# Ranking a hybrid decoder's side TensorE work 30 instructions behind its place

## The chip, the cores and the metric

The kernel runs on one core of one Trainium2 chip. A core has a matrix engine (TensorE; PE in the profile, PEld for its weight loads), a vector engine (VectorE, DVE), a scalar engine (ScalarE, ACT), GpSimd (POOL), and SyncE (SP), whose queue issues nearly all DMA transfers here. TensorE writes into PSUM banks. The metric is device time of one launch in microseconds: 2443.29 us, the median of three runs (2434.94, 2443.29 and 2444.47).

## The reference

One layer of a hybrid decoder trunk: a prompt of 2048 tokens and eight sample tokens (one new token each, with caches), width 1024, in float32. Cut to what matters:

```
h    = rms_norm(x, norm1_w)
q, k, v, z, xbc, dt_raw = split(h @ w_in)
a    = sliding-window attention(q, k, v)        # window 128, sinks, relative bias
xbc  = silu(causal_conv(xbc)); xs, B, C = split(xbc)
s    = chunked state-space scan(xs, dt, B, C)   # chunks of 128, state carried on
s    = group_rms_norm((s + xs * D) * silu(z))
x    = x + concat(a, s) @ w_out
h2   = rms_norm(x, norm2_w)
x    = x + (silu(h2 @ w_gate) * (h2 @ w_up)) @ w_down
y    = rms_norm(x, final_norm_w)
```

Beside y, the last window of keys and values, the last convolution rows and the scan's state are returned.

## The kernel before

Tokens are cut into six groups: 2, 3, 3, 3, 3 and 2 blocks of 128 (256 or 384 columns), the last with the eight sample tokens (264 columns). Every activation lies with features on partitions and tokens along the free axis. For accuracy each float32 factor of a projection is split into a rounded high part and a remainder, and three products are summed: high by high, high by low, low by high. So one 128-feature output tile of a 1024-deep projection is 24 matmuls into one PSUM bank (`proj`, L232, `mm3`). A weight tile comes in two halves of 512 KB from a copy that an earlier group has stored already split (tile `w`, tag `w2`, five buffers, L203), or, when first met, as raw 256 KB halves (`wraw`, L206) that ScalarE rounds (L207) and GpSimd or VectorE subtracts (L210); the split pair is stored for later groups (L214).

The work of a group is written as stages, Python generators that emit some instructions and yield:

- I and X load the tokens and form the normed, split pair (I for group 0, X for the others);
- A projects x, B, C and dt and runs the convolution; K projects keys and values; B projects q and z;
- P is attention, Q the scan and its group norm, Y the sample tokens: together the mixers;
- S splits the mixers' output; O is the output projection with the residual; H the second norm; F the FFN, 44 gate and up units with the down projections between them; Z the final norm and the store of y.

A norm's sum over partitions is a matmul with a matrix of ones (`rinv_b`, L683), whose ScalarE and VectorE steps (L693 to L701) then give the factor.

`run` (L1067) steps one main stage a unit at a time, and after each unit lets side stages advance by a given number of steps. `tick` (L188) first emits work that `later` (L185) has set down as due: evictions, the dt rows and sums, transposes of v. In the steady state F of group i is the main stage, with the mixers of group i+1 (spread over `RM` = 53 units) and X of group i+2 beside it; then K and A of group i+2 with S of group i+1 and Z of group i; then O of group i+1; then B of group i+2 with H of group i+1 (L1116 to L1131). Before group 0's F, the groups are filled in by hand (L1101 to L1115). In the last but one F, the S, O and H of the last group are side stages too (L1130).

The order in which each engine executes is not the order of emission. The kernel is built in a tile context with `schedule_with_timeline_sim=True`: every emitted instruction gets the next rank (the context's `cur_priority`), and a planner, which plays the program on a model of the machine, gives each engine the ready instruction of lowest rank. That order is then fixed; on the chip each engine works through its own list and waits at semaphores. Main projections use the PSUM tag `d` (four banks, `psd` in the profile), mixers and norms the tag `m` (four banks, `psm`). The mixers' small buffers share tag `m2` (eight), and x1 and the convolution's tile share tag `x1` (two).

```
    V, S, G, PE, SP = nc.vector, nc.scalar, nc.gpsimd, nc.tensor, nc.sync
    def mm(o, l, r, start=True, stop=True):
        PE.matmul(o, l, r, start=start, stop=stop)
```

All matmuls go through `mm` and so have one line, L104; transposes are `PE.transpose` at L426, L473, L608, L728, L735 and in Y.

Of the kernel before, what the change touches and what calls it, by code (L numbers as in the profile page):

```python
# [27 lines left out]
UQ = 5  # L28
RH0 = 3
DM = 1024  # L30
KT = DM // P
NH = 8
EPS = 1e-6
# [30 lines left out]
def ff_chunks(nf):  # L64

    r = [list(range(f, min(f + FC, nf))) for f in range(0, nf, FC)]
    if len(r) > 1 and len(r[-1]) == 1:
        r[-2:] = [r[-2] + r[-1]]
    return r


@with_exitstack
def hymba(ctx: ExitStack, tc: tile.TileContext, I: dict, O: dict, groups):
    nc = tc.nc
# [4 lines left out]
    chunks = ff_chunks(NF)  # L79
    c_off = [c[0] * DM for c in chunks]  # L80

# [6 lines left out]
    def T(shape, dtype=F32, tag=None, bufs=1):  # L88
        cnt[0] += 1
        nm = f"{tag}_{cnt[0]}"  # L90
        return sb.tile(shape, dtype, tag=tag, name=nm, bufs=bufs)

    def PS(tag):
        cnt[0] += 1
        return pp.tile([P, 512], F32, tag=tag, name=f"ps{tag}_{cnt[0]}", bufs=4)
# [2 lines left out]
        cnt[0] += 1  # L98
        return dr.tile(shape, F32, tag=tag, name=f"{tag}_{cnt[0]}", bufs=bufs)

    V, S, G, PE, SP = nc.vector, nc.scalar, nc.gpsimd, nc.tensor, nc.sync

    def mm(o, l, r, start=True, stop=True):
        PE.matmul(o, l, r, start=start, stop=stop)  # L104
# [65 lines left out]

    wdr = T([P, KT, NH], tag="wdr")
    wdt = T([P, KT, 2 * NH], F32R, tag="wdt")

# [14 lines left out]
    def tick():  # L188
        clock[0] += 1
        now = sorted((d for d in due if d[0] <= clock[0]), key=lambda d: d[:2])  # L190
        due[:] = [d for d in due if d[0] > clock[0]]
        for d in now:
            d[2]()
# [31 lines left out]
    def mm3(o, w, x, k, N, start, stop):  # L225
        whi, wlo = w
        xhi, xlo = x
        mm(o, whi, xhi[:, k, :N], start, False)
        mm(o, whi, xlo[:, k, :N], False, False)
        mm(o, wlo, xhi[:, k, :N], False, stop)  # L230

    def proj(w, x, N, bank="d"):  # L232
        ps = PS(bank)
        for k in range(KT):
            mm3(ps[:, :N], w[k], x, k, N, k == 0, k == KT - 1)
        return ps

    def act_pair(home):
        return tuple(T([P, KT, NMAX], F32R, tag=home + part) for part in ("hi", "lo"))

# [26 lines left out]
    def stage_x(g):  # L267
        N, off = g["N"], g["off"]
        x = g["x"] = act_pair("a")
        xr = T([P, KT, NMAX], tag="xr")  # L270
        for h in range(2):
# [4 lines left out]
        yield from squares(xr, sq, N)  # L276
        yield from rinv_b(sq, N, DM)
        yield from scaled(xr, S_N1, sq, N, x, lambda m: xr[:, m, :N])


    def stage_x0(g):
# [18 lines left out]
        for m in range(KT):  # L300
# [3 lines left out]
            if m % 4 == 3:  # L304
                yield
        yield from rinv_b(r, N, DM)

# [15 lines left out]
    def squares(x, sq, N):  # L323
        t = None
        for m in range(KT + 1):
            if t is not None:
                total(sq, t, N)
            t = T([P, NMAX], tag="tmp", bufs=6) if 0 < m < KT else None
            if m < KT:
                square(x, m, sq if m == 0 else t, N)  # L330
            yield

    def scaled(x, c, r, N, pair, to):

        ts = {}

        def low(m):
            e = G if m % 2 else V
            e.tensor_tensor(pair[1][:, m, :N], ts[m], pair[0][:, m, :N].bitcast(F32), ALU.subtract)  # L339

        for m in range(KT + 2):
            if m >= 2:
                low(m - 2)
            if 1 <= m <= KT:
                S.activation(pair[0][:, m - 1, :N], ts[m - 1], AF.Copy)
            if m < KT:
                ts[m] = to(m)
                V.scalar_tensor_tensor(ts[m], x[:, m, :N], col(c, m), r[:, :N], ALU.mult, ALU.mult)  # L348
            yield
# [333 lines left out]
    def rinv_b(ss, N, d):  # L683

        ss = [s[:, :N] for s in (ss if isinstance(ss, list) else [ss])]
        ps = []
        for s in ss:
            ps.append(PS("m"))
            mm(ps[-1][:, :N], ones, s)
        yield  # L690
        v = [T([P, NMAX], tag="tmp", bufs=6)[:, :N] for _ in ss]
        for s, p in zip(ss, ps):
            S.activation(s, p[:, :N], AF.Ln, bias=epsc[:, 0:1], scale=1.0 / d)  # L693
        for s, u, p in zip(ss, v, ps):
            S.activation(u, p[:, :N], AF.Copy, bias=-0.5 * EPS, scale=-0.5 / d)
            S.activation(s, s, AF.Exp, scale=-0.5)  # L696
        yield
        for s, u in zip(ss, v):
            V.tensor_tensor(u, u, s, ALU.mult)
            V.tensor_tensor(u, u, s, ALU.mult)  # L700
            V.scalar_tensor_tensor(s, u, 1.5, s, ALU.add, ALU.mult)  # L701
        yield
# [262 lines left out]
    def stage_h(g):  # L965
        N, x1, sq = g["N"], g["x1"], g["sq"]
        while g.get("nsq", 0) < KT:
            yield
        yield from rinv_b(sq, N, DM)
        h2 = g["h2"] = act_pair("a" if g is gs[-1] else "b")  # L970
# [65 lines left out]
    def stage_z(g):  # L1036
        N, x1, sq, off = g["N"], g["x1"], g["sq"], g["off"]
        while g.get("nsq", 0) < 2 * KT:
            yield
        yield from rinv_b(sq, N, DM)  # L1040
        for m in range(KT):
# [19 lines left out]
    def step(c, i):  # L1061

        if (c, i) not in made:
            made[c, i] = kinds[c](gs[i])
        return next(made[c, i], 0)

    def run(main, *rest, units=None, drain=99):  # L1067


        rest = [e if isinstance(e, list) else [list(e[0]), e[1], 0.0] for e in rest]  # L1070

        def advance(e, k):
            e[2] += k
            while e[2] >= 1 and e[0]:
                if step(*e[0][0]) == 0:
                    e[0].pop(0)
                e[2] -= 1

        while units is None or units > 0:
            says = step(*main) if main else 0  # L1080
            if says in (0, "tail"):
                break
            tick()
            for e in rest:
                advance(e, e[1])
            if units is not None:
                units -= 1
        while any(e[0] for e in rest[:drain]):
            for e in rest[:drain]:
                e[2] = 0.0  # L1090
                advance(e, 1)
            tick()
        return rest[drain:]

    def mixers(i, u):
# [3 lines left out]
        return r + ([([("Y", i)], 55 / (0.8 * u))] if g["smp"] else [])  # L1099

    run(("I", 0), units=1)  # L1101
    setup_consts()
    tabd = setup_bias()
    run(("A", 0), ([("I", 0)], RI), units=UA)
    bscr = spread_bias(tabd)
    r = run(("A", 0), ([("X", 1)], RX1), drain=0)
    r = run(("K", 0), *r, drain=0)
    load_bias(bscr)
# [115 lines left out]
```

## Time and profile before

| what | value |
|---|---|
| median of three runs | 2443.29 us |
| the profiled execution: time, span | 2437.1 us, 2434.7 us |
| TensorE busy, weight loads busy | 2314.5 us, 2244.4 us |
| VectorE, ScalarE, GpSimd busy | 1250.4, 875.1, 814.4 us |
| TensorE matmuls | 14633 |
| mean granted TensorE clock | 0.985 |
| HBM traffic | 516.67 MB read, 110.21 MB written, 257 GB/s over the span |

Times in the views are counted in microseconds from the span's start. A line of a timeline has start, length, engine, line, operation, out<-in and count, and in brackets the idle time of the engine before it and what ended that. A line of waits has the waiter, what it waited for, the total in us, how many times, and the longest.

### The profile page before, as it was taken

How to read it: one execution, taken by the hardware profiler on the slowest of the kernel's cores; microseconds unless marked ns; L12 is line 12 of the kernel's file. 1: busy time of each engine (PE TensorE's matmuls, PEld its weight loads, DVE VectorE, ACT ScalarE, POOL GpSimd, SP SyncE). 2: the span in 40 equal slices, each digit the busy share in tenths (PEclk: the TensorE clock that was granted, in tenths of full speed). 3: DMA queues.
4: the chain of work that ended last, by engine and by line, in shares of the span. 5: the costliest groups of instructions: out<-in, count | busy, mean ns of one | idle time of the engine just before them, and what ended most of it. 6: DMA issues, size and time to landing. Idle time of an engine off the chain costs nothing.

```text
span 2434.7 us, 39664 instructions
## 1 busy us (share of the span) xinstructions
PE 2314.5 (95%) x14633; PEld 2244.4 (92%) x14633; DVE 1250.4 (51%) x2526; ACT 875.1 (36%) x1861; POOL 814.4 (33%) x884
## 2 busy tenths in 40 slices
PE   6889898999999999999999999999999999999997
PEld 5779887889999999999999999999989999999997
DVE  8895978564556545344653533453354544233223
ACT  5665556454434434333432422132233212121001
POOL 5555766553444434223322312231123132111000
PEclk9899998999999999999999999999999999999999
DMA  8648575787776777878788887777789788888997
GB/s 276 221 151 284 186 239 195 248 306 272 252 247 212 243 246 278 272 262 277 242 281 285 269 250 243 238 215 240 237 308 301 230 280 270 249 294 306 332 339 259
DMA packets 227227, 628.97 MB, mean 258 GB/s; under 512 B 24323, under 2 KB 57916, under 8 KB 226892
## 3 DMA queue, kind: packets, MB, share of 16 engines
q1 hardware_dynamic: 226892, 626.26, 77.5%
q8 instruction: 116, 1.90, 0.3%
q14 instruction: 75, 0.61, 0.1%
q10 hardware_dynamic: 144, 0.20, 0.0%
HBM read 516.67 MB, written 110.21 MB: 257 GB/s over the span
## 4 chain that ended last, share of the span: by engine, by line
PE 68%; DMA 7%; DVE 2%; ACT 1%; issue 0%; SPq 0%; ACTq 0%; POOL 0%; DVEq 0%
PE psd L104 64%; PE psm L104 4%; DMA w<-wd 2%; DMA w<-wi 2%; DMA w<-wu 1%; DMA w<-wg 1%; DVE x L1042 1%; DVE xr L348 1%; DVE alo L339 0%; DMA out_yT_dram<-x 0%; DMA m<-sbcd 0%; PE psm L608 0%; PE psm L728 0%; DVE w L210 0%; ACT L696 0%
## 5 line engine op out<-in xcount | busy, mean ns | idle before, releaser
L104 PE MATMUL psd<-bhi,w 128*128 128x384 f32 (+1 forms) x4448 | 1097.4, 328 | 40.0 <-DVE w L210 14.9
L104 PEld LDWEIGHTS psd<-bhi,w 128*128 128x128 f32 x4448 | 785.6, 190 | 54.6 <-DVE w L210 19.1
L104 PE MATMUL psd<-blo,w 128*128 128x384 f32 (+1 forms) x2224 | 720.8, 324 | 0.7 <-DVE blo L339 0.6
L104 PE MATMUL psd<-hc,w 128*128 128x384 f32 (+2 forms) x3168 | 527.5, 323 | 28.6 <-DMA w<-wd 9.8
L104 PEld LDWEIGHTS psd<-hc,w 128*128 128x128 f32 x3168 | 502.5, 191 | 43.3 <-issue 12.4
L104 PE MATMUL psd<-ahi,w 128*128 128x384 f32 (+1 forms) x2272 | 516.7, 314 | 22.4 <-DMA w<-wi 8.4
L104 PEld LDWEIGHTS psd<-blo,w 128*128 128x128 f32 x2224 | 423.2, 190 | 2.8 <-DVE blo L339 1.1
L104 PEld LDWEIGHTS psd<-ahi,w 128*128 128x128 f32 x2272 | 386.1, 189 | 31.2 <-DMA w<-wi 5.0
L210 POOL TENSOR_TENSOR w<-wraw,w 128x512 fp32r<-128x512 f32 (+1 forms) x195 | 252.7, 1298 | 382.1 <-ACT w L207 346.3
L104 PE MATMUL psd<-alo,w 128*128 128x384 f32 (+1 forms) x1136 | 354.9, 312 | 0.0
L207 ACT ACTIVATE w<-wraw 128x512 fp32r<-128x512 f32 (+1 forms) x391 | 232.5, 601 | 324.4 <-PE psd L104 187.7
L994 DVE TENSOR_TENSOR x<-psd,x 128x384 f32<-128x384 f32 (+2 forms) x336 | 168.0, 510 | 193.9 <-PE psd L104 193.4
L104 PEld LDWEIGHTS psd<-alo,w 128*128 128x128 f32 x1136 | 215.2, 189 | 1.3
L210 DVE TENSOR_TENSOR w<-wraw,w 128x512 fp32r<-128x512 f32 (+1 forms) x196 | 164.4, 840 | 90.7 <-ACT w L207 88.6
L1009 POOL TENSOR_TENSOR hc<-tmp,hc 128x384 fp32r<-128x384 f32 (+2 forms) x66 | 67.6, 1025 | 356.8 <-ACT hc L1005 356.7
L1001 DVE SCALAR_TENSOR_TENSOR tmp<-tmp,psd 128x384 f32<-128x384 f32 (+2 forms) x132 | 66.7, 505 | 233.2 <-ACT tmp L1015 233.0
L1015 ACT ACTIVATE tmp<-psd 128x384 f32<-128x384 f32 (+2 forms) x132 | 59.7, 452 | 349.4 <-PE psd L104 349.2
L321 POOL TENSOR_TENSOR sq<-sq,tmp 128x384 f32<-128x384 f32 (+2 forms) x112 | 109.7, 979 | 199.4 <-ACT tmp L318 194.4
L1004 DVE SCALAR_TENSOR_TENSOR tmp<-psd,tmp 128x384 f32<-128x384 f32 (+2 forms) x132 | 67.4, 511 | 199.1 <-PE psd L104 198.8
L1005 ACT ACTIVATE hc<-tmp 128x384 fp32r<-128x384 f32 (+2 forms) x132 | 64.4, 488 | 270.4 <-DVE tmp L1004 267.0
L382 DVE SCALAR_TENSOR_TENSOR x<-tmp,cols,x 128x384 f32<-128x384 f32 (+1 forms) x144 | 100.3, 700 | 37.2 <-ACT x L404 26.7
L318 ACT ACTIVATE tmp<-x 128x384 f32<-128x384 f32 (+2 forms) x84 | 40.5, 489 | 137.5 <-DVE x L942 100.4
(269 smaller groups left out, 2145.3 us busy)
## 6 DMA issues: line engine op xcount, KB each, us to landing
w<-wu SPq DMA_DIRECT2D x177, 512.0 KB, 5.0
w<-wg SPq DMA_DIRECT2D x175, 512.0 KB, 4.5
w<-wi SPq DMA_DIRECT2D x144, 512.0 KB, 4.6
w<-wd SPq DMA_DIRECT2D x192, 384.0 KB, 3.8
w<-wo SPq DMA_DIRECT2D x65, 512.0 KB, 4.6
wraw<-in_wg_dram SPq DMA_DIRECT2D x89, 256.0 KB, 4.3
wu<-w SPq DMA_DIRECT2D x44, 512.0 KB, 3.3
wg<-w SPq DMA_DIRECT2D x44, 512.0 KB, 3.7
```

The costliest lines, as they stand in the source:

```text
L104: PE.matmul(o, l, r, start=start, stop=stop)
L207: S.activation(hi, raw, AF.Copy)
L210: e.tensor_tensor(lo, raw, hi.bitcast(F32), ALU.subtract)
L318: S.activation(t[:, :N], x[:, m, :N], AF.Square)
L321: e.tensor_tensor(sq[:, :N], sq[:, :N], t[:, :N], ALU.add)
L382: V.scalar_tensor_tensor(acc, raw[:, j:j + NP], cwc(j, t), acc, ALU.mult, ALU.add)
L994: V.tensor_tensor(x1[:, m, :N], p[:, :N], x1[:, m, :N], ALU.add)
L1001: V.scalar_tensor_tensor(t[:, :N], t[:, :N], 1.0, pg[:, :N], ALU.add, ALU.mult)
L1004: V.scalar_tensor_tensor(t[:, :N], pu[:, :N], 0.5, t[:, :N], ALU.mult, ALU.mult)
L1005: S.activation(hh[:, 0, :N], t[:, :N], AF.Copy)
L1009: e.tensor_tensor(hl[:, 0, :N], t[:, :N], hh[:, 0, :N].bitcast(F32), ALU.subtract)
L1015: S.activation(t[:, :N], pg[:, :N], AF.Tanh, scale=0.5)
```

## The change

TensorE is wrapped in a small class. While `PE.places` is 30, the rank counter is raised by 30 for the instruction that is issued and lowered again behind it, so this instruction has a rank 30 above the one that its place would give it, and those that follow on other engines keep theirs. `places` is 30 in `run` while due work (`tick`) and side stages (`advance`) are emitted after a main unit, and 0 for the main stage, for the drain loop at the end of `run`, and for everything outside `run`. So the mixers' TensorE instructions are covered, and with them those of the norms in I, X, H and Z, the dt and v transposes and sums that are due, and the last group's output projection, where O is a side stage.

```
+PLACES = 30
...
+class Behind:
+
+
+    def __init__(self, tc, engine):
+        self.tc, self.engine, self.places = tc, engine, 0
+
+    def __getattr__(self, op):
+        f = getattr(self.engine, op)
+
+        def issue(*a, **k):
+            rank = self.tc.cur_priority
+            self.tc.cur_priority = rank + self.places
+            f(*a, **k)
+            self.tc.cur_priority -= self.places
+
+        return issue
+
...
-    V, S, G, PE, SP = nc.vector, nc.scalar, nc.gpsimd, nc.tensor, nc.sync
+    V, S, G, PE, SP = nc.vector, nc.scalar, nc.gpsimd, Behind(tc, nc.tensor), nc.sync
...
             says = step(*main) if main else 0
             if says in (0, "tail"):
                 break
+            PE.places = PLACES
             tick()
             for e in rest:
                 advance(e, e[1])
+            PE.places = 0
             if units is not None:
                 units -= 1
```

## The prediction

> **What bounds the kernel now.** I read the page's busy shares first, then the kernel cut into its stages, then TensorE's waits, whole and for the long middle stretch.
>
> ```profile
> PE 2314.5 (95%) x14633; PEld 2244.4 (92%) x14633; DVE 1250.4 (51%) x2526; ACT 875.1 (36%) x1861; POOL 814.4 (33%) x884
> ```
>
> TensorE is busy 95% of the 2434.7 us span; only about 120 us of it are idle. No order of the same matmuls can return more than part of that, so the place of the idle time matters:
>
> ```profile
> 0.00:100.00 100.00, 71.69 (x462) 63.69 (x462) 79.95 (x157) 55.64 (x113) 51.87 (x63) 0.90 0.76 253
> 100.00:237.00 137.00, 126.86 (x793) 118.70 (x792) 99.48 (x195) 81.43 (x178) 75.45 (x84) 0.96 0.66 222
> 237.00:545.00 308.00, 272.24 (x1984) 252.92 (x1984) 228.81 (x418) 168.88 (x366) 190.61 (x183) 0.97 0.70 232
> 545.00:1770.00 1225.00, 1216.23 (x7138) 1196.61 (x7138) 592.97 (x1198) 434.93 (x903) 381.38 (x419) 1.00 0.77 252
> 1770.00:2210.00 440.00, 427.58 (x2672) 418.59 (x2671) 187.55 (x419) 104.85 (x242) 104.93 (x126) 0.99 0.84 277
> 2210.00:2434.70 224.70, 199.90 (x1592) 193.85 (x1590) 61.63 (x141) 29.39 (x63) 10.17 (x13) 0.98 0.89 314
> ```
>
> The columns are the stretch, its length, then busy time of TensorE, its weight loads, VectorE, ScalarE and GpSimd, and the granted clock. Idle TensorE: 28.3 us up to 100 us, 10.1 us up to 237 us (where the first FFN starts), 35.8 us in the first group's FFN, then 8.8 us in 1225 us, 12.4 us, and 24.8 us in the last FFN, which has no mixers beside it. The middle half of the kernel is a TensorE stream without holes. These are the waits of it there (first five lines) and those of the whole kernel that a mixers' or norms' matmul (PSUM tag m) ends:
>
> ```profile
> PE psd L104 <- DMA w<-wd: 3.9, 3, 1.8
> PE psd L104 <- DMA w<-wi: 2.8, 2, 1.9
> PE psd L104 <- DMA w<-wu: 1.5, 1, 1.5
> PE psd L104 <- DVE tmp L1001: 0.4, 1, 0.4
> PE psd L104 <- DVE w L210: 0.2, 1, 0.2
> ...
> PE psm L104 <- DVE dt L261: 4.3, 2, 4.0
> PE psm L104 <- DVE sq L321: 1.6, 1, 1.6
> PE psm L104 <- DVE m L622: 1.6, 2, 1.4
> PE psm L608 <- POOL big L603: 1.4, 3, 0.7
> PE psm L104 <- DVE m L732: 1.3, 1, 1.3
> PE psm L104 <- DVE m L628: 0.4, 1, 0.4
> PE psm L104 <- ACT m L548: 0.2, 1, 0.2
> ```
>
> In the middle no matmul of tag m waits at all. In the whole kernel they wait 10.8 us; the 1.6 us for sq are the last norm, which runs without a main stage and so is not shifted. **The direct prize is at most 9.2 us**, all of it before 545 us.
>
> **The change, part by part.** It adds and removes no instruction. While due work and side stages are emitted, each TensorE instruction gets a rank 30 higher; all others, DMAs included, keep theirs. The planner takes, among ready instructions of an engine, the lowest rank, so up to 30 later instructions' worth of main matmuls pass a shifted one, if they are ready too. One projection unit is 24 matmuls:
>
> ```profile
> 641.40 4.18 PE psd L104 x24
> ```
>
> That is 0.174 us each, so the shift is at most 30 x 0.174 = 5.2 us. The 30 ranks also count the unit's two to six weight instructions and what the rest of the side step emits, so I take 12 to 20 matmuls, 2 to 3.5 us. PSUM banks and SBUF buffers of these matmuls are held that much longer.
>
> *Middle, mixers:* nothing to gain (no wait above). To lose: the last mixers' matmul of a group and the output projection that needs it stand at
>
> ```profile
> 918.64 0.61 PE L104 MATMUL psm<-m,vs 128*128 128x512 f32 x2
> 983.22 0.34 PE L104 MATMUL psd<-bhi,w 128*128 128x384 f32 x1
> ```
>
> 64 us apart, so 5.2 us later is hidden by the K and A projections between. Without that cover each of four groups would pay up to 5.2 us. I take 0.
>
> *First unit chain (A of group 0):* the norm's matmul is shifted, and the evictions that free TensorE's four banks wait for it.
>
> ```profile
> 19.63 0.60 PE L104 MATMUL psm<-hc,cst 128*128 128x256 f32 x2
> 24.31 0.28 PE L104 MATMUL psd<-bhi,w 128*128 128x256 f32 x1
> 26.03 0.35 PE L104 MATMUL psd<-bhi,w 128*128 128x256 f32 x1 [1.44 <-DVE tmp L363]
> 2333.97 16.14 PE psd L104 x130
> ```
>
> From its start to the last main matmul before the wait are 24.31 - 19.63 = 4.68 us; at 0.124 us (16.14/130, at 264 columns the nearest row) that is 36 main matmuls beside its own two, so the norm stands 12 into a unit. Thirty ranks less three ScalarE and some seven weight instructions leave place 20: 8 x 0.124 = **+1.0 us**, all on the path because TensorE already waits 1.44 us for it (bounds 0 and 12 x 0.124 = 1.5).
>
> *First FFN's start:* the same with the norm ahead of it.
>
> ```profile
> 228.79 0.59 PE L104 MATMUL psm<-sq,cst 128*128 128x256 f32 x2
> 236.50 0.40 PE L104 MATMUL psd<-bhi,w 128*128 128x256 f32 x2
> 237.49 0.39 PE L104 MATMUL psd<-blo,w 128*128 128x256 f32 x1 [0.59 <-DVE blo L339]
> ```
>
> From 228.79 to 236.50 us some 42 matmuls of K1's 48 run beside its own two (7.71/0.174), so it stands 6 into K1's first unit; 30 less six instructions of its own stage and six of weights make place 18: 12 x 0.174 = **+2.1 us**. The FFN's first matmuls already wait 0.59 us, so this lengthens the wait (bounds 0, and 18 x 0.174 = 3.1).
>
> *Final norm of a group (Z) under K and A:* its chain ends in a TensorE wait:
>
> ```profile
> 935.74 0.34 PE L104 MATMUL psd<-ahi,w 128*128 128x384 f32 x1
> 941.63 0.66 PE psm L104 x2
> 946.99 5.09 DVE x L1042 x8
> 952.11 4.10 DMA out_yT_dram<-x
> 957.33 9.02 DMA w<-wi
> 966.49 0.42 PE L104 MATMUL psd<-ahi,w 128*128 128x384 f32 x1 [0.92 <-DMA w<-wi]
> w<-wi SPq DMA_DIRECT2D x144, 512.0 KB, 4.6
> ```
>
> The y store frees x1, whose reload (L939) is issued on SP's queue ahead of a weight, which then lands after 9.02 instead of 4.6 us. K begins at 935.74, so 5.89/0.174 = 33 matmuls precede the norm: 9 into K's second unit. 30 less three and six puts it at 21, 12 x 0.174 = 2.1 us later. Behind the waiting store on SP stand the weights' loads. Three groups have this; if all of it reaches TensorE it is +6.3, if the planner moves the reload past one weight, 0. I take the middle, **+3.0 us**.
>
> *Last group's output projection as side work:* its 24 matmuls per step now alternate with the next FFN unit's, so four of the five weight buffers are in use at once. Half of that stretch is 12 x (0.174 + 0.124) = 3.6 us for a load that takes 4.6 us, but the fifth buffer covers a half unit of 1.5 us: **0** (bounds 0 and 3 boundaries x 1.0 = 3).
>
> *Waits removed:* before 237 us mixers are emitted densely, 15 units for all steps, and the step's other instructions use up most of the 30 ranks; also an in-order engine that stops waiting there meets VectorE at 99.5 of 137 us. Of 9.2 us I take **-2** (bounds -9.2 and 0).
>
> Sum: 1.0 + 2.1 + 3.0 + 0 - 2 = +4.1 us; bounds -9.2 and 1.5 + 3.1 + 6.3 + 3 = +13.9. The profiled execution took 2437.1 us, 6.2 below the median of the runs. The four executions known (2434.94, 2437.1, 2443.29, 2444.47) average 2440.0; plus 4.1 gives **2444 us**.
>
> What a longer hole costs besides itself the trace shows:
>
> ```profile
> 390.79 0.55 PE L104 MATMUL psd<-hc,w 128*128 128x256 f32 x1 [4.80 <-ACT ahi L345]
> 391.00:396.00 5.00, 3.53 (x14) 2.97 (x15) 5.00 (x8) 3.29 (x7) 4.27 (x4) 0.50 0.26 79
> 396.00:402.00 6.00, 6.00 (x32) 5.68 (x32) 6.00 (x11) 4.76 (x8) 2.51 (x2) 0.62 0.65 185
> ```
>
> After 4.80 us idle the clock stood at 0.50 for 5 us and 0.62 for 6, some 2.5 + 2.3 = 4.8 us of work lost. The hole that I expect at the first FFN is 0.6 + 2.1 = 2.7 us. The Trainium skill, TensorE: Matmul & The Clock Gate, section "HAM oscillation — how this bites in real kernels", forbids idle gaps over about 3.4 us; by it 2.7 us cost only themselves and the sum stays. If the norm passes the whole unit, the hole is 0.6 + 3.1 = 3.7 us, and by that rule the clock falls.
>
> **Rivals.** (1) *Nothing moves that matters:* where the planner's TensorE is starved the order is by readiness, where it is full there is slack: +0, 2440 us. For it: no tag-m wait in the middle. Against: the two norm chains with waits behind them. (2) *Slower through SP's queue:* the late Z chain puts the x1 reload ahead of weights that TensorE needs at once. Each of three groups then waits a full extra landing, 9.02 - 4.6 = 4.4 us, 13.3 in all, with the two first norms 16.4: 2456 us. It decides when the norm passes K's last matmul, so that SP holds a second weight. For: the wait is already there. Against: weights may go ahead of the reload. (3) *Faster in the first FFN:* there TensorE idles 35.8 us because weight splits share VectorE, ScalarE and GpSimd with the mixers' steps. With matmuls later the mixers' bursts move off the splits; a third of 35.8 with half of the 9.2 us is -16.5: 2424 us. For: VectorE is busy 229 of 308 us. Against: those bursts keep their ranks and size. (4) *The clock falls at the first FFN,* a hole of 3.7 us with 4.8 us of lost work: 3.1 + 4.8 + 1.0 + 3.0 - 2 = +9.9: 2450 us.
>
> **How the numbers follow.** Forecast 0.45, rival 1 0.18, rival 2 0.17, rival 3 0.15, rival 4 0.05. A measurement of this kernel can tell about 0.5%, 12.2 us around 2443.29, from no change. Faster by more: rival 3, and little of the forecast's lower bound (2431): 0.17. Slower by more than 12.2 (over 2455.5): half of rival 2 by itself, and what the scatter of executions (2434.94 to 2444.47) lifts over it of the forecast's upper end (2454), of rival 2 and of rival 4: 0.18. Between: 0.65. The forecast's own range is 2431 to 2454; taking in rival 2 and part of rival 3 and the scatter, the range is 2426 to 2460.
>
> **What would show it.** Right: the two norm matmuls stand about 1 and 2 us later against the main matmuls, tag-m matmuls stand inside units instead of at their ends, and TensorE is idle 8 to 16 us from 545 to 1770 us. The 3.98 us dt wait stays or shrinks. Wrong: TensorE's idle time in the first FFN changes by more than 10 us, or the middle grows new waits of the mixers.

## The result, and the profile after

| | before | after |
|---|---|---|
| median, lowest to highest | 2443.88 us, 2434.94 to 2446.01 (4 runs) | 2467.99 us, 2462.20 to 2469.63 (4 runs) |
| profiled execution: time, span | 2437.1, 2434.7 us | 2469.63, 2467.6 us |

The ratio is 1.0101 with a 95% interval of 1.0071 to 1.0132: the change costs 24 us, and the time lies above the predicted range (2426 to 2460). Of the profile of the changed kernel, first the page's line of busy times. All matmuls now have line L85, inside the wrapper; line numbers behind it are higher by 19.

```profile
PE 2343.4 (95%) x14633; PEld 2254.7 (91%) x14633; DVE 1250.4 (51%) x2526; ACT 879.0 (36%) x1863; POOL 812.9 (33%) x884
```

TensorE is busy for 2343.4 us instead of 2314.5, with the same 14633 matmuls, and idle for 2467.6 - 2343.4 = 124.2 us instead of 120.2. So 28.9 of the 32.9 us between the two spans are busy time, and 4.0 idle time. (These two executions lie 32.9 us apart, the medians 24.1.) Most of the lost time is not counted as waiting: the same matmuls take longer. The stretches of the changed kernel, with the columns of the table of before:

```profile
0.00:100.00 100.00, 73.00 (x456) 65.28 (x456) 77.84 (x147) 53.21 (x107) 51.86 (x62) 0.90 0.74 243
100.00:237.00 137.00, 126.64 (x780) 118.86 (x779) 96.97 (x197) 80.31 (x176) 75.96 (x82) 0.95 0.67 227
237.00:545.00 308.00, 276.09 (x1990) 257.02 (x1989) 225.31 (x421) 172.61 (x372) 188.65 (x184) 0.95 0.69 228
545.00:1770.00 1225.00, 1212.02 (x7007) 1175.47 (x7007) 587.38 (x1184) 430.48 (x887) 372.52 (x412) 1.00 0.76 250
1770.00:2210.00 440.00, 423.48 (x2642) 412.45 (x2641) 187.24 (x411) 103.97 (x240) 103.26 (x121) 1.00 0.82 270
2210.00:2467.60 257.60, 232.21 (x1767) 225.60 (x1765) 75.65 (x168) 38.40 (x83) 20.66 (x24) 0.98 0.88 303
```

The fourth row is the one to read. In the same 1225 us TensorE is idle 13.0 us (8.8 before) at the same granted clock of 1.00, yet it starts 7007 matmuls instead of 7138. One takes 1212.02/7007 = 0.1730 us instead of 1216.23/7138 = 0.1704. For 7138 of them that makes 18.5 us. The loss is thus in the middle, where TensorE is full and the prediction saw 64 us of slack. The first matmul of the output projection (O) of group 1 and that of group 4 mark three equal rounds of the loop, first of before, then of after:

```profile
560.08 0.34 PE L104 MATMUL psd<-bhi,w 128*128 128x384 f32 x1
1819.45 0.34 PE L104 MATMUL psd<-bhi,w 128*128 128x384 f32 x1
```

```profile
563.55 0.34 PE L85 MATMUL psd<-bhi,w 128*128 128x384 f32 x1
1846.86 0.34 PE L85 MATMUL psd<-bhi,w 128*128 128x384 f32 x1
```

These three rounds take 1283.3 us instead of 1259.4: 23.9 of the 32.9 us. Up to their start the changed kernel is only 3.5 us late, and behind them it loses 5.5 us more.

**Where a matmul got longer.** The groups of TensorE and of its weight loads for one operation, the diagonal product of the scan (`yd` in the mixers' stage Q, `psm<-big,m`): eight heads per block of tokens, each a matmul with 64 weight columns (`128*64`), written to the lower or the upper 64 partitions. In the trace each is two passes, so 16 small matmuls per block, 256 in 16 blocks. First before, then after:

```profile
L104 PE MATMUL psm<-big,m 128*64 128x128 f32 x256 | 21.8, 283 | 0.0
L104 PEld LDWEIGHTS psm<-big,m 128*64 128x64 f32 x256 | 14.6, 136 | 6.8 <-issue 4.5 <-DVE m L749 0.5 <-DVE hc L638 0.4
```

```profile
L85 PE MATMUL psm<-big,m 128*64 128x128 f32 x256 | 36.1, 291 | 0.0
L85 PEld LDWEIGHTS psm<-big,m 128*64 128x64 f32 x256 | 18.2, 135 | 15.0 <-issue 12.7 <-DVE hc L657 0.4 <-PE psm L85 0.4
```

The same 256 small matmuls are busy for 36.1 us instead of 21.8, and ahead of their weight loads PEld stands idle for 15.0 us instead of 6.8; for 12.7 us of it (4.5 before) the profile shows nothing that it waits for ("issue"). The timeline of TensorE and its weight loads shows why. Before, one block's product:

```profile
775.22 0.34 PE L104 MATMUL psd<-bhi,w 128*128 128x384 f32 x1
775.48 1.09 PE L104 MATMUL psm<-big,m 128*64 128x128 f32 x16
776.51 0.44 PE L104 MATMUL psd<-bhi,w 128*128 128x384 f32 x1
776.79 0.34 PE L104 MATMUL psd<-blo,w 128*128 128x384 f32 x1
```

After, part of one block's product (PEld rows are the weight loads):

```profile
785.32 0.19 PEld L85 LDWEIGHTS psm<-big,m 128*64 128x64 f32 x2 [0.25 <-issue]
785.32 0.43 PE L85 MATMUL psm<-big,m 128*64 128x128 f32 x2
...
785.68 0.19 PEld L85 LDWEIGHTS psd<-bhi,w 128*128 128x128 f32 x1 [0.17 <-issue]
785.68 0.45 PE L85 MATMUL psd<-bhi,w 128*128 128x384 f32 x1
786.06 0.19 PEld L85 LDWEIGHTS psm<-big,m 128*64 128x64 f32 x2 [0.19 <-issue]
786.06 0.43 PE L85 MATMUL psm<-big,m 128*64 128x128 f32 x2
...
786.42 0.44 PE L85 MATMUL psd<-blo,w 128*128 128x384 f32 x1
```

Before, all 16 stand in one piece between two main matmuls. From 775.22 to 776.79 are 1.57 us for two main matmuls (0.174 each) and the 16: 1.22 us for the product, 0.15 per head. After, the heads and the main unit's matmuls take turns. One round of a head and a main matmul is 786.42 - 785.68 = 0.74 us, 0.56 more than the main matmul alone. At each change between a main matmul and a head, either way, the weight load starts only in the moment in which its matmul starts. Within a head it does not: the load of the second pass stands ahead of its matmul, behind the first pass.

```profile
785.37 0.14 PEld L85 LDWEIGHTS psm<-big,m 128*64 128x64 f32 x1
785.48 0.27 PE L85 MATMUL psm<-big,m 128*64 128x128 f32 x1
```

**So a head that stands alone costs 0.41 us more than a head in a piece.** Counted along TensorE's order, the 16 products lie in 30 pieces before (7 of them lone heads) and in 74 after (53 lone heads). Take the stretches of TensorE's order from the matmul before a piece to the start of the second one behind it, each matmul counted once where stretches overlap, and take off 0.174 us for each matmul that is not the product's. That leaves 27.5 us for the product before and 45.8 after, +18.3. In the three rounds it is 12.3 and 30.5: +18.2 of their 23.9 us. TensorE's idle time there grows from 14.0 to 19.9 us, +5.9. So about three quarters of the rounds' loss are the product, one quarter is waiting.

Why they take turns: a raised instruction keeps a rank that is only 30 on. The heads are emitted one after the other with consecutive ranks, and the next main unit's matmuls, emitted right behind the step, get consecutive ranks over the same numbers. Two lists of consecutive ranks over the same numbers merge one by one; block30 and ydm200 below test this reading.

### The profile page after: what moved, and what is told of

Read it like the earlier page. It is cut to its first block, busy times and chain, and to the rows that moved or that the text cites. A ratio compares the mean times of both kernels' runs of the same rounds, so it can differ in the third digit from the quotient of the medians.

```text
span 2467.6 us, 39689 instructions
## 1 busy us (share of the span) xinstructions
PE 2343.4 (95%) x14633; PEld 2254.7 (91%) x14633; DVE 1250.4 (51%) x2526; ACT 879.0 (36%) x1863; POOL 812.9 (33%) x884
## 4 chain that ended last, share of the span: by engine, by line
PE 64%; DMA 8%; DVE 3%; POOL 1%; ACT 1%; issue 1%; SPq 0%; ACTq 0%; DVEq 0%; POOLq 0%
PE psd L85 60%; PE psm L85 4%; DMA w<-wu 2%; DMA w<-wi 2%; DMA w<-wd 1%; DMA w<-wg 1%; DVE x L1061 1%; DMA m<-sbcd 1%; DVE xr L367 1%; DMA out_yT_dram<-x 1%; DVE alo L358 0%; POOL m L914 0%; DMA m<-in_sssm_dram 0%; DMA wd<-w 0%; DVE m L917 0%
## 5 line engine op out<-in xcount | busy, mean ns | idle before, releaser
L85 PE MATMUL psd<-bhi,w 128*128 128x384 f32 (+1 forms) x4448 | 1110.6, 330 | 33.6 <-DVE w L229 11.5
L85 PEld LDWEIGHTS psd<-bhi,w 128*128 128x128 f32 x4448 | 789.1, 191 | 52.8 <-DVE w L229 13.9
L85 PE MATMUL psd<-blo,w 128*128 128x384 f32 (+1 forms) x2224 | 726.1, 327 | 0.4 <-DVE blo L358 0.4
L85 PE MATMUL psd<-hc,w 128*128 128x384 f32 (+2 forms) x3168 | 544.9, 325 | 29.4 <-DMA w<-wd 11.1
L85 PEld LDWEIGHTS psd<-hc,w 128*128 128x128 f32 x3168 | 504.1, 191 | 46.2 <-issue 15.9
L85 PE MATMUL psd<-ahi,w 128*128 128x384 f32 (+1 forms) x2272 | 520.9, 316 | 23.2 <-DMA w<-wi 10.9
L85 PEld LDWEIGHTS psd<-blo,w 128*128 128x128 f32 x2224 | 425.0, 191 | 4.2 <-issue 1.9
L85 PEld LDWEIGHTS psd<-ahi,w 128*128 128x128 f32 x2272 | 389.0, 190 | 32.6 <-DMA w<-wi 8.9
L85 PE MATMUL psd<-alo,w 128*128 128x384 f32 (+1 forms) x1136 | 355.9, 313 | 0.0
L85 PEld LDWEIGHTS psd<-alo,w 128*128 128x128 f32 x1136 | 216.3, 190 | 1.5 <-issue 0.4
```

What stands on the lines that cost most here:

```text
L85: f(*a, **k)
```

## The experiments

Two theories. **Theory 1, taking turns:** the loss comes from side matmuls that are dealt out singly among main ones, the scan's diagonal product above all. **Theory 2, lateness:** it comes from mixers and norms that are later than before and hold buffers and banks longer. All twelve kernels were timed beside the kernel before on the same chip. "Product's pieces" and "side pieces" are counted along TensorE's order in the trace (the product alone; all matmuls of tag m); busy is TensorE's line of each page; rounds is the time from O of group 1 to O of group 4 in the one profiled execution, and the last column is the product's time in them by the sum above.

| kernel | against before, us (median) | ratio, 95% | TensorE busy | product's pieces | side pieces | three rounds | product in the rounds |
|---|---|---|---|---|---|---|---|
| before | | | 2314.5 | 30 | 251 | 1259.4 | 12.3 |
| after | +24.1 | 1.0071 to 1.0132 | 2343.4 | 74 | 572 | 1283.3 | 30.5 |
| noyd | +3.6 | 1.0000 to 1.0037 | 2324.1 | 24 | 522 | 1262.2 | 13.7 |
| block30 | +13.2 | 1.0035 to 1.0065 | 2328.8 | 35 | 380 | 1264.8 | 16.3 |
| p10 | +20.3 | 1.0061 to 1.0117 | 2338.6 | 79 | 549 | 1280.9 | 35.2 |
| p60 | +37.9 | 1.0132 to 1.0168 | 2350.9 | 83 | 589 | 1279.9 | 35.7 |
| ydonly | +25.5 | 1.0076 to 1.0132 | 2341.2 | 72 | 293 | 1280.3 | 31.1 |
| normonly | +0.9 | 0.9993 to 1.0018 | 2317.4 | 28 | 248 | 1258.7 | 12.8 |
| wide | +12.7 | 1.0038 to 1.0081 | 2329.5 | 76 | 587 | 1271.6 | 16.3 |
| wide0 | -1.0 | 0.9982 to 1.0008 | 2311.6 | 33 | 253 | 1260.1 | 16.1 |
| m30 | +25.0 | 1.0090 to 1.0127 | 2346.3 | 88 | 581 | 1285.9 | 37.0 |
| ydm200 | -10.7 | 0.9949 to 0.9974 | 2310.3 | 23 | 248 | 1255.5 | 11.9 |
| ydorder | +3.4 | 1.0003 to 1.0025 | 2321.7 | 29 | 251 | 1261.2 | 16.9 |
| mix | +7.0 | 1.0005 to 1.0031 | 2317.0 | 19 | 498 | 1264.1 | 13.2 |

Over these kernels the change of the rounds' time follows the product's time in them within 4 us. Two are further off: the changed kernel itself, with 5.7 us more, and wide, with 8.2 us more. In both TensorE's idle time in the rounds grows too, by over 5 us.

**The shift without the product (noyd).** Against the changed kernel:

```
         yd = PS("m")
+        places, PE.places = PE.places, 0
         for h in range(NH):
             mm(yd[...], xdt[:, h, :], csb[:, h, :])
+        PE.places = places
```

> Edit: the changed kernel with the shift off for one kind of side matmul only, the scan's eight matmuls per block with 64 weight columns (psm<-big,m, 256 of the 970 side matmuls). Theory 1 (taking turns costs, and most for these, 48 of which went from 3.4 to 6.6 us in a group): 3.3 us and up to 1 us of main matmuls around them back in five groups, 13 to 20 us, so 2448 to 2455 us. Rival (lateness of the whole chain): a quarter of the matmuls earlier gives at most a quarter of 24 us back, 2462 to 2468 us.

Measured: 2441.53 us, +3.6 on the kernel before, better than my band of 2448 to 2455. Unshifting one operation of eight instructions per block gives back 20 of 24 us, though 522 of the 572 side pieces are still there. Other side matmuls dealt out singly cost little.

**The product alone (ydonly),** with every other TensorE instruction at its old rank:

```
             PE.side = PLACES          # in run, and 0 behind the side stages; places stays 0
...
+        PE.places = PE.side
         for h in range(NH):
             mm(yd[...], xdt[:, h, :], csb[:, h, :])
+        PE.places = 0
```

> Only the scan's diagonal product (8 small matmuls per block, 64 weight columns, psm<-big,m) keeps the shift of 30; every other TensorE instruction has its old rank. Theory 1 (turn-taking breaks this product up): nearly the whole loss is here, +16 to +19 us on the kernel before, about 2455, with the product's matmuls standing by twos between main matmuls as in the changed kernel. Theory 2 (lateness of the mixers and norms as a whole): one product of 16 blocks late is little, within 4 us of the kernel before.

Measured: 2463.43 us, +25.5 (+18.5 to +32.2 by the interval), 6 us over the expected band. Page line and the product's group:

```profile
PE 2341.2 (95%) x14633; PEld 2256.4 (91%) x14633; DVE 1260.7 (51%) x2526; ACT 874.3 (35%) x1861; POOL 816.9 (33%) x884
```

```profile
L85 PE MATMUL psm<-big,m 128*64 128x128 f32 x256 | 35.8, 291 | 0.0
```

One operation, whose rows are 1% of TensorE's work, makes the whole loss, as far as the intervals tell: busy 2341.2 against the changed kernel's 2343.4, the product 35.8 against 36.1 us. In the rounds ydonly loses 20.9 us, of which the product takes 18.8, and waiting nothing (14.0 us idle, as before). Noyd and ydonly together settle where the loss is.

**One rank for a whole side step (block30),** so that its TensorE instructions are not spread over 30 numbers:

```
-            self.tc.cur_priority = rank + self.places
+            if self.places and self.block is None:
+                self.block = rank + self.places
+            self.tc.cur_priority = self.block if self.places else rank
             f(*a, **k)
-            self.tc.cur_priority -= self.places
+            self.tc.cur_priority = rank + 1
...             # block is set back to None ahead of each due item and each step of a stage
```

> Edit: all side TensorE instructions of one emission step get one and the same rank, 30 above the first of them, so they are as late as in the changed kernel but stay together instead of taking turns one by one with the main matmuls. In the planned order the stretches of side matmuls fall from 572 to 380 (251 before). Theory 1 (taking turns costs TensorE time, some 5 to 7 us in each of the groups): most of the loss goes, 2448 to 2454 us, and from 563 to 1847 us the yd matmuls (psm<-big,m) take 3.4 us per group again instead of 6.6. Rival (the mixers are late, and buffers are held longer): the delay is the same, so 2463 to 2470 us as after the change.

Measured: +13.2. The product is back to 35 pieces and costs 24.2 us in its group; the three rounds lose 5.4 us instead of 23.9. The first instruction of each step is shifted as far as in the changed kernel, those behind it somewhat less, so this run alone does not part the two theories; m30 below does. The product makes 4.0 of the 5.4 us. What is left of the loss lies outside the rounds and isn't explained by the product.

**Shifts of 10 and 60 (p10, p60):** `PLACES = 10`, `PLACES = 60`.

> Edit: 10 places instead of 30. The planned order has 549 stretches of side matmuls, nearly the 572 of 30 places, with a third of the delay. Theory 1 (cost per change of sides): 2460 to 2468 us. Rival (cost per place of delay): a third of 24 us, about 2452 us.

> Edit: 60 places instead of 30. The planned order has 589 stretches of side matmuls with twice the delay. Theory 1 (cost per change of sides): 2465 to 2474 us. Rival (cost per place of delay): twice 24 us, about 2492 us.

Measured: 2458.25 us, +20.3, and 2475.85 us, +37.9. Each lies 2 us outside theory 1's band and further from the rival's number. A third of the shift makes nearly all of the loss, and in the three rounds 10, 30 and 60 cost 21.5, 23.9 and 20.5 us: with the product broken into 74 to 83 pieces, the size of the shift hardly matters there. Only p60 adds something, behind the rounds: from O of group 4 to the end it takes 631.0 us, p10 614.4, before 615.2. That part fits lateness; which work is late there I did not follow up.

**The shift with its sign turned (m30):** `PLACES = -30`. Nothing is late any more, but the ranks again lie over those of a main unit, the one before.

> The changed kernel with the sign turned: the same TensorE instructions get a rank 30 ahead of their place (PLACES = -30), so nothing is late. Theory 1 (turn-taking at equal ranks): they now tie with what is left of the main unit emitted before, the planner lets them take turns again, and the loss is of the same size, +18 to +30 us on the kernel before, with the scan's diagonal product again by twos. Theory 2 (lateness): no loss, at or under the kernel before.

Measured: 2463.69 us, +25.0. Its timeline:

```profile
1156.07 0.43 PE L85 MATMUL psm<-big,m 128*64 128x128 f32 x2
1156.43 0.45 PE L85 MATMUL psd<-bhi,w 128*128 128x384 f32 x1
1156.80 0.43 PE L85 MATMUL psm<-big,m 128*64 128x128 f32 x2
```

The same turns at the same 0.73 us a round, with the mixers early instead of late. Theory 2 can't make this loss.

**The product far ahead (ydm200):** ydonly with `PLACES = -200`, where no open main matmul has such a rank.

> Only the scan's diagonal product is moved, 200 ranks ahead of its place: no main matmul still open has such a rank, so it goes in one piece as soon as its operands are there. Theory 1: it stands in one stretch of 16 matmuls in nearly all of the 16 blocks, which by the kernel before's own stretches (1.23 us extra for one of 16, 27.6 us in all) saves 27.6 - 16 x 1.23 = 8 us at most; I expect -2 to -8 us. Theory 2: no difference.

Measured: 2427.99 us (2424.36 to 2429.12), ratio 0.9962: the only kernel here that is clearly faster than the one before. Page line, and one block's product:

```profile
PE 2310.3 (95%) x14633; PEld 2244.5 (93%) x14633; DVE 1249.6 (52%) x2526; ACT 875.1 (36%) x1861; POOL 817.9 (34%) x884
```

```profile
765.41 1.09 PE L85 MATMUL psm<-big,m 128*64 128x128 f32 x16
766.43 0.44 PE L85 MATMUL psd<-bhi,w 128*128 128x384 f32 x1
766.71 0.33 PE L85 MATMUL psd<-blo,w 128*128 128x384 f32 x1
```

In 13 of 16 blocks the product is one piece (9 before). The sign was as expected, the size at its far end or past it: the pieces themselves save 27.5 - 24.4 = 3.1 us by the sum used above. TensorE's busy time falls by 4.2 us and its idle time from 120.2 to 112.3, in profiled executions that scatter by several us. Why the idle time falls stays open.

**Both together (mix):** the changed kernel with the product at -200, shown against noyd.

```
-        places, PE.places = PE.places, 0
+        places, PE.places = PE.places, -200
```

> The changed kernel, shift of 30 for all side TensorE work, except that the scan's diagonal product stands 200 ranks ahead of its place. Theory 1, if its parts add: noyd's cost on the kernel before (+3.6 us) and ydm200's gain (-10.7 us) give -7 us, about 2432; the norms and the other mixers' matmuls are as late as in the changed kernel. Theory 2 (lateness): the product is one of some ten kinds of shifted matmuls, so most of the 24 us stays, over 2455.

Measured: 2445.08 us, +7.0, so 17 us better than the changed kernel, each against its own kernel before, and far from theory 2's 2455; but the parts don't add, and I was 13 us off. With a span of 2445.7 us, TensorE is idle 128.7 us (120.2 before) and, by the table, busy only 2.5 us longer. What the shift still costs here is mostly waiting, the small part that theory 2 does explain.

**Half width or the turn itself (wide, wide0).** The same edit in the changed kernel (wide) and in the kernel before (wide0): each small matmul takes both heads' 128 weight columns and writes all 128 partitions. The second head's result overwrites the first's: this kernel leaves out the diagonal product of half of the heads, and serves for its time alone.

```
-            mm(yd[(h % 2) * 64:(h % 2) * 64 + 64, ...], xdt[:, h, :], csb[:, h, :])
+            q = h // 2
+            mm(yd[:, q * P:(q + 1) * P], xdt[:, 2 * q:2 * q + 2, :].rearrange("p a b -> p (a b)"), csb[:, h, :])
```

> The changed kernel, all shifted, but each small matmul of the scan's diagonal product takes both heads' 128 weight columns instead of its own 64, and writes all 128 partitions (the second head's overwrites the first's, so the diagonal part of the scan is left wrong; as many matmuls, of twice the width). Taken against wide0, the same edit without the shift. If what makes a turn dear is the half width (loads that are not pulled ahead, two heads that no longer run side by side), the shift costs 4 to 9 us here instead of 24. If it is the turn itself, 20 us or more as before.

> The kernel before with the same edit as in wide (128 weight columns per head's matmul, the diagonal part of the scan wrong). The two heads cannot run side by side on the two halves of the columns any more. If a pair of halves costs 109 ns and a full-width pass about 70 to 110 ns, 16 blocks times 16 passes add 16 x 16 x 0.015 to 0.055 = 4 to 14 us to the kernel before.

Measured: wide +12.7, wide0 -1.0: the shift costs 13.7 us at full width, against 24 to 25. That is outside my band of 4 to 9 and under the 20 of the rival, and each side has several us of uncertainty. Wide0 was to cost 4 to 14 us; full width alone costs nothing that the times show. Timelines of wide, TensorE and its loads:

```profile
782.31 0.43 PE L85 MATMUL psd<-bhi,w 128*128 128x384 f32 x1
782.39 0.37 PEld L85 LDWEIGHTS psm<-big,m 128*128 128x128 f32 x2
782.58 0.38 PE L85 MATMUL psm<-big,m 128*128 128x128 f32 x2
...
782.72 0.42 PE L85 MATMUL psd<-blo,w 128*128 128x384 f32 x1
```

As many turns as in the changed kernel (76 pieces), but a round takes 782.72 - 782.31 = 0.41 us instead of 0.74: the head's load starts at 782.39, 0.19 us ahead of its matmul at 782.58, where the half-width load behind a main matmul started with its own matmul. By the sum used above the product takes 29.6 us in wide and 29.6 in wide0: turns cost nothing at full width and 18.3 us at half width. So it is not the turn that is dear, but the change of width in it. All of wide's loss lies outside the product. In the rounds wide takes 11.5 us more than wide0, and 4.7 of these are idle time (19.4 against 14.7). Noyd and mix, with the product out of the turns, lose 3.6 and 7.0 us; the rest of wide's loss stays open.

The Trainium skill, TensorE: Matmul & The Clock Gate, "Step-by-step: what each phase is for", says that TensorE pulls weight loads ahead of running matmuls when row groups don't conflict or the load goes to the background buffer. Loads behind a matmul of their own width agree: 0.19 us ahead at full width in wide, 0.11 us at half width for the second pass of a head (785.37 and 785.48 above). Loads behind a matmul of the other width did not do so (0.00 us ahead in the changed kernel's turns). The same page's "Part 3: Packing small matmuls — row/col tiling" says for tiles that a load overlaps running matmuls only when the row group differs. The loads of the second passes do not bear that out, since all matmuls here use the same 128 rows (`128*64`, `128*128`), and the measurement decides. No run here shows why a change of width holds the load back.

**The two heads side by side (ydorder):** the kernel before with `for h in (0, 2, 4, 6, 1, 3, 5, 7)`, so that neighbours write the same half of the columns.

> The kernel before with the eight heads of the diagonal product in the order 0, 2, 4, 6, 1, 3, 5, 7, so that neighbouring matmuls write the same half of the columns. No shift. If two heads side by side are what makes a stretch cheap, a stretch of 16 grows from 1.1 us to 16 x 0.1 = 1.6 us or more, +7 to +14 us over 16 blocks. If the loss of a turn is only in the change between main and half-width matmuls, within 3 us of the kernel before.

Measured: +3.4 (1.0003 to 1.0025), between the two bands. A piece of 16 grows from 1.23 to 1.71 us, as the median over nine of each; that is 0.03 us per small matmul, and the product's sum grows from 27.5 to 34.5 us. So two heads on the two halves do run partly side by side, worth 0.06 us a head or somewhat more: in the new order, too, the trace shows the first heads of the second half starting beside the last ones of the first half. Against the 0.41 us that a head loses in turns this is a small share.

**The norms alone (normonly):** only the ones-matmul of `rinv_b` is shifted.

> Only the ones-matmul of the norms (rinv_b) keeps the shift of 30. The prediction's terms for it (first unit chain +1.0, first FFN +2.1, final norm under K and A up to +3.0) give +3 to +6 us on the kernel before, about 2441 to 2444; theory 1 expects no more than that here, since two full-width matmuls between main ones cost little. Theory 2 (lateness, the norm chains above all) expects most of the 24 us here, over 2455.

Measured: +0.9 (-1.7 to +4.4 by the interval). That cannot be told from no change, and it leaves out theory 2's number and the +6 of the prediction's three terms together.

## Why the prediction was wrong

**The step that failed** is "*Middle, mixers*: nothing to gain ... I take 0". The 64 us of slack held: after still has no wait of a tag-m matmul from 545 to 1770 us, and ydonly and p10 lose their 21 us in the rounds with no more idle time than before. But I priced only when a mixers' matmul runs, not next to what. I had the mixing in sight twice: "tag-m matmuls stand inside units instead of at their ends" was to show me right, and for the last group's output projection I wrote that its matmuls would alternate. Each time a matmul cost its row's duration wherever it stood. What the runs put there is 256 small matmuls that cost 0.15 us a head in one piece and 0.56 us alone: +18.2 us in the three rounds by the trace, and +25.5 us (18.5 to 32.2) for ydonly's launch, where they alone are shifted.

The first reading of the profile led there. "TensorE is busy 95% ... no order of the same matmuls can return more than part of that" is true for gains. I took it for the losses too, as if busy time were fixed and only idle time could move. The busy time depends on the order: of the 28.9 us by which it grew here, 18.3 are the product's stretches. What made up the rest was not followed up.

The signs that the prediction named could not show this either. Most of those for being right came: tag-m matmuls inside units (572 side pieces for 251), and 13.0 us idle from 545 to 1770 us, where 8 to 16 were named. One failed: the longest dt wait grew by 0.5 us (below). Neither of those for being wrong came. They watch places, waits and idle time; none watches TensorE's busy time, where most of the loss was.

The other steps, with the rows of after:

```profile
20.47 0.59 PE L85 MATMUL psm<-hc,cst 128*128 128x256 f32 x2
26.52 0.36 PE L85 MATMUL psd<-bhi,w 128*128 128x256 f32 x1 [1.43 <-DVE tmp L382]
...
242.06 0.51 PE L85 MATMUL psd<-bhi,w 128*128 128x256 f32 x2 [1.81 <-ACT bhi L364]
...
978.69 0.42 PE L85 MATMUL psd<-ahi,w 128*128 128x384 f32 x1 [1.49 <-DMA w<-wi]
```

- *First unit chain* (+1.0): the norm passed 3 main matmuls, not 8, and the wait stayed as it was (1.44 and 1.43 us). The 0.49 us by which the waiting matmul is later were there five main matmuls ahead of the norm's old place. So this term came out at nothing.
- *First FFN's start* (+2.1): the norm passed 11 main matmuls where 12 were expected, the wait grew from 0.59 to 1.81 us, and the FFN's matmuls lost 1.7 us against those ahead of them. Right, and a little smaller.
- *Final norm Z* (+3.0 for three groups): the norm passed 3 main matmuls, not 12. The wait for the weight in this group grew from 0.92 to 1.49 us. All waits for such weights from 545 to 2210 us grew from 8.4 to 10.9 us, near the forecast, but normonly, with the norm in the same place, has 7.6: not clear of the scatter. Normonly, with all three terms in it, shows +0.9 us where they add to +6.1.
- *Waits removed* (-2): the sign was wrong. The waits of tag-m matmuls in the whole kernel grew from 10.8 to 20.0 us:

```profile
PE psm L85 <- DVE dt L280: 7.6, 2, 4.5
PE psm L85 <- DVE m L751: 4.8, 2, 3.4
PE psm L85 <- POOL big L622: 2.3, 3, 1.2
```

  Waiting for dt grew from 4.3 to 7.6 us, the longest such wait from 4.0 to 4.5, so my sign that the 3.98 us wait "stays or shrinks" failed. TensorE's waits for other things shrank meanwhile; its whole idle time grew by 4.0 us.
- *Last group's output projection* (0): not tried by itself. TensorE's idle time from 1770 to 2210 us, where it stands, grew from 12.4 to 16.5 us, but other shifted work stands there too.

**The rivals.** (1) *Nothing moves:* true for the mixers' waits in the middle, not for the order. (2) *SP's queue:* in the group read above the wait grew by 0.57 us, not 4.4; one later wait for such a weight is 4.02 us long (1840.85 us; the longest before is 2.25), but the 13.3 us in all did not come. (3) *Faster in the first FFN:* its idle time went from 35.8 to 31.9 us in the same window, the right direction, by 3.9 us instead of a third, and its granted clock fell from 0.97 to 0.95. (4) *The clock falls at the first FFN:* not at its start; the hole there was 1.81 us. It fell 15 us later, at a mixers' wait that grew. Timeline and stretches of after:

```profile
257.25 0.74 PE L85 MATMUL psm<-m,big 128*128 128x256 f32 x4 [3.41 <-DVE m L751]
```

```profile
257.00:262.00 5.00, 4.75 (x27) 4.75 (x28) 5.00 (x18) 2.72 (x6) 4.73 (x4) 0.66 0.32 108
```

The same two views of before, at the same place:

```profile
254.71 0.36 PE L104 MATMUL psd<-bhi,w 128*128 128x256 f32 x1 [2.60 <-DVE tmp L1001]
```

```profile
257.00:262.00 5.00, 5.00 (x45) 5.00 (x44) 4.30 (x14) 1.99 (x5) 4.01 (x4) 1.00 0.79 297
```

Behind 3.41 us of waiting the clock stood at 0.66 for 5 us, 1.7 us of work lost; behind 2.60 us it had stayed at 1.00. The Trainium skill's rule of about 3.4 us, cited in the prediction, agrees with both, but not with another place of before, where the clock fell behind a shorter hole:

```profile
1798.47 0.39 PE L104 MATMUL psd<-ahi,w 128*128 128x264 f32 x1 [2.25 <-DMA w<-wi]
1799.98:1806.80 6.82, 5.83 (x25) 5.27 (x24) 3.77 (x24) 1.21 (x4) 0.31 (x2) 0.50 1.03 396
```

So the prediction's step from a hole of 2.7 us to "cost only themselves" was not safe, though at the first FFN's start the clock held.

Every rival, like the forecast, was about when work happens. None was about the order inside a full engine, so the range could not hold the result.

## What to carry to other kernels

Before shifting work on a full engine, ask what its instructions will stand between. A rank shift of fixed size lays one run of consecutive ranks over another, and the planner deals them out one by one; matmuls of another width than those around them then lose the piece in which they were cheap, as the half-width ones did here. Keep such a group in one piece, by ranks that no open work shares, and read TensorE's busy time, not only its idle time, to see whether it worked.

## What the runs showed of the hardware

- A head, two passes with 64 weight columns, costs 0.56 us alone between two full-width matmuls and 0.15 us in a piece of 16 passes. At a change of width, either way, the weight load starts only with its own matmul (785.32 and 785.68 in the rows above); behind a pass of the same width it starts ahead (0.11 us at half width, 0.19 us at full width in wide). With 128 weight columns in the same turns the round takes 0.41 instead of 0.74 us.
- So in turns the half-width form is dearer than the full-width one: by the sum over its stretches the product takes 45.8 us at half width (after) and 29.6 at full width (wide), while mostly in whole pieces the two are close, 27.5 us (before) and 29.6 (wide0).
- Two neighbouring half-width matmuls on different column halves gain at least 0.06 us a head over two on the same half (1.23 against 1.71 us for 16).
